# A modulation row written into the attention loop, and another way out of PSUM for the two halves of the attention output

## The chip, the cores and the metric

The kernel runs on one core of a Trainium2 chip. The metric is the device time of one execution in microseconds (us); the time of a kernel is the median of its runs. Five engines work side by side, each in the order of its own instruction queue: TensorE (PE in the profile; its weight loads are PEld), VectorE (DVE), ScalarE (ACT), GpSimd (POOL) and SyncE (SP), whose queue here issues most of the DMAs. Matmul results go to PSUM, everything else lies in SBUF.

## The reference

The reference is a two-layer encoder for one sequence of 1024 tokens and 1024 channels in fp32. Layer 0 has attention (16 query heads, 4 key and value heads of 64), layer 1 a Hyena convolution; both end in a feed-forward block with a depthwise convolution. What matters here is layer 0's modulation and its attention:

```python
mod = (c_act @ ada_w[i] + ada_b[i])[:, None, :]
sh1, sc1, g1, sh2, sc2, g2 = jnp.split(mod, 6, axis=-1)
h = rmsnorm(x, norm1_g[i]) * (1.0 + sc1) + sh1
...
s = jnp.einsum('bqkgd,bskd->bkgqs', q_blk, k, preferred_element_type=jnp.float32) * scale
p = jax.nn.softmax(s, axis=-1).astype(v.dtype)
return jnp.einsum('bkgqs,bskd->bqkgd', p, v)
...
x = x + g1 * y
h = rmsnorm(x, norm2_g[i]) * (1.0 + sc2) + sh2
x = x + g2 * conv_ffn(h, ...)
```

Of the six modulation rows of layer 0, `sh1` and `sc1` (rows 0 and 1) are needed before attention, `g1` (row 2) when attention's result is added to `x`, and rows 3 to 5 later still.

## The kernel before

**Number format.** An fp32 product is made of matmuls on fp32r parts: each operand is split into a high part (a cast on ScalarE) and a low part (the difference, a subtraction on VectorE, `sub_lo`, L162), and products of the parts are added up in PSUM.

**The projection (L757 to L792).** Queries, keys and values are computed in three chunks of 512 columns (`ch` 2, then 0, then 1), each for eight tiles of 128 tokens. TensorE fills a PSUM tile `qkv_mm`; VectorE and ScalarE normalise it and apply the rotary tables (`rope_norm`, L713 to L722, whose tiles are `qk_n`, `qk_a`, `qk_b`); TensorE transposes the result, and SP stores the queries to DRAM (`qd`). The weights come through two buffers called `w_raw`.

**Modulation rows on GpSimd.** `mod_step(i, acc, k)` (L185) loads 512 KB of `ada_w` into one of the same two `w_raw` buffers (SP, L187), multiplies it by a scalar per partition on GpSimd (L189 for k = 0, which writes `acc`; L191 otherwise) and adds it to `acc` (GpSimd, L192). `acc` is always the tile `ssq`. Eight steps make a row. `mod_fin` (L209) adds up `ssq` over the partitions with eight one-column matmuls (L212, 16 in the profile) and adds the bias on VectorE (`mod_bias`, L203); only then can the next row start to write `ssq`. Rows 0 and 1 and those of layer 1 are dot products on VectorE (`mod_dot`), the last of which read `ssq` as a row of activated conditions before row 2 begins. The eight steps of row 2 are written at the head of chunk `ch == 1` (L770).

**Attention (L811 to L938).** The work is cut into 32 units `u` (a key head g = u // 8 and a block of 128 queries, for the group's four query heads), each of eight key blocks `sb`. The loop counts `n` over all 256 pairs (u, sb), plus a lag of 2. Round n has, in written order:

- for sb = 0, `finish(u, 0)`: the reciprocal of the softmax sums (VectorE, L883), spread by GpSimd into `rbs` (L885);
- `transp` (TensorE transposes four tiles of probabilities into `pt_ps`, L854, three buffers), `pt_hi` (ScalarE, L859) and `pt_lo` (VectorE, L162, tile `pT_lo`);
- `attend` of the pair two rounds back: two matmuls into `o_ps` (L872, L873). `o_ps` has one buffer, a [128, 512] tile: the stationary operand `vst` holds high and low parts of the values side by side, so that partitions 0 to 63 get one half of the output and partitions 64 to 127 the other, and the output is their sum;
- when that pair was its unit's last, `finish(u, 2)` and `finish(u, 3)` (below);
- at set rounds a `mod_step` or a `mod_fin` for rows 3 to 5;
- for sb < 4, the scores of one head of the next unit: four matmuls into `s_ps` (L830, L831, two buffers), their row maximum `nmx` on VectorE (L838), the exponential `p_t` on ScalarE (L848).

`finish(u, 2)` moves both halves out of PSUM with four ScalarE copies of [64, 256] (L893): the even and the odd heads of the first half into the lower and the upper 64 partitions of `o_s`, the same of the second half into `o_l`. `finish(u, 3)` adds the two on VectorE (L895, [128, 256], both inputs in SBUF), transposes `rbs` into PSUM (L899, tile `rb_ps`), multiplies (VectorE, L900), and GpSimd writes high and low parts of the result (L902, L903).

**The order.** In the projection and in attention the queues are not ordered by hand. A scheduler builds the whole program at once: it takes written order as priority and lets every engine take the first instruction that can run by its own estimate of times. On each engine, on the chip, that order is then fixed.

**The rounds of the rows.** `LAG, MOD0, MODD = 2, 27, 9` (L905): with i, k = divmod((n - 27) // 9, 8), step k of row 3 + i is written at n = 27, 36, 45 and so on, one per nine key blocks, and `mod_fin` of a row six rounds after its last step: at n = 24 (row 2), 96, 168 and 240. At n = 246 the first weight tile of the output projection is loaded and split through `w_raw` (L927).

After attention, the output projection follows (`wo_y`), then the feed-forward block and layer 1.

Of the kernel before, what the change touches and what calls it, by code (L numbers as in the profile page):

```python
# [7 lines left out]
F32 = mybir.dt.float32  # L8
# [6 lines left out]
P = 128  # L15
D = 1024
L = 1024
KT = D // P
# [3 lines left out]
HD = 64  # L22
# [93 lines left out]
def tile_kernel(ctx: ExitStack, tc: tile.TileContext, t: dict):  # L116
    nc = tc.nc
    mm = nc.tensor.matmul
    V = nc.vector
    ADD, SUB, MUL = ALU.add, ALU.subtract, ALU.mult  # L120
# [64 lines left out]
    def mod_step(i, acc, k):  # L185
        raw = raw_tile()
        nc.sync.dma_start(raw, t["ada_w"][i - 2, k])  # L187
        if k == 0:
            nc.gpsimd.tensor_scalar(acc, raw, csil[:, 0:1], None, op0=MUL)  # L189
        else:  # L190
            nc.gpsimd.tensor_scalar(raw, raw, csil[:, k:k + 1], None, op0=MUL)  # L191
            nc.gpsimd.tensor_tensor(acc, acc, raw, op=ADD)  # L192
# [507 lines left out]
    with tc.tile_pool(name="qkv", bufs=1) as qp:  # L700
        def qtile(tag, bufs):
            return qp.tile([P, 8, HD], F32, name=tag, tag=tag, bufs=bufs)

        def stats(pv, nh):
            sq = qtile("qk_sq", 2)
            nc.scalar.activation(sq[:, 0:nh], pv, AF.Square)
            ss = qp.tile([P, 8], F32, name="qk_ss", tag="qk_ss", bufs=3)
            V.tensor_reduce(ss[:, 0:nh], sq[:, 0:nh], op=ADD, axis=AX.X)
            nc.scalar.activation(ss[:, 0:nh], ss[:, 0:nh], AF.Sqrt, bias=eps, scale=1.0 / HD)
            V.reciprocal(ss[:, 0:nh], ss[:, 0:nh])  # L710
            return ss

        def rope_norm(pv, nh, nm, j, ss):  # L713
            qn, A, B = qtile("qk_n", 2), qtile("qk_a", 2), qtile("qk_b", 2)
            V.tensor_tensor(qn[:, 0:nh], pv, ss[:, 0:nh].unsqueeze(2).to_broadcast([P, nh, HD]), op=MUL)
            V.tensor_tensor(A[:, 0:nh], qn[:, 0:nh], T[nm, 0][:, j:j + 1, :].to_broadcast([P, nh, HD]), op=MUL)
            for hf in range(2):
                a, b = slice(32 * hf, 32 * hf + 32), slice(32 - 32 * hf, 64 - 32 * hf)
                V.tensor_tensor(B[:, 0:nh, a], qn[:, 0:nh, b],
                                T[nm, 1][:, j:j + 1, a].to_broadcast([P, nh, 32]), op=MUL)  # L720
            V.tensor_tensor(A[:, 0:nh], A[:, 0:nh], B[:, 0:nh], op=ADD)
            return A  # L722

        def flat(ap):
            return ap.bitcast(F32).rearrange("p a d -> p (a d)")

        def k_tile(pv, ss, j):
            ts = slice(j * P, (j + 1) * P)
            nc.scalar.copy(vst[j][:, :, 0, :], pv[:, NKV:2 * NKV])
            sub_lo(vst[j][:, :, 1, :], pv[:, NKV:2 * NKV], vst[j][:, :, 0, :])  # L730
            kr = rope_norm(pv[:, 0:NKV], NKV, "k", j, ss)
            st = qp.tile([P, 2, NKV, 2, HD], F32R, name="k_st", tag="st", bufs=2)
            kin = kr[:, 0:NKV].unsqueeze(2)
            nc.scalar.copy(st[:, 0, :, 0:1, :], kin)
            sub_lo(st[:, 1, :, 0:1, :], kin, st[:, 0, :, 0:1, :])
            nc.scalar.copy(st[:, :, :, 1, :], st[:, :, :, 0, :].bitcast(F32))
            for i, dst in enumerate((kTh, kTl)):
                tp = mt("qkv_tr", "tr")
                for g in range(NKV):
                    nc.tensor.transpose(tp[:, g * P:(g + 1) * P], flat(st[:, i, g]), ident)  # L740
                for g in range(NKV):
                    nc.scalar.copy(dst[g][:, ts], tp[:, g * P:(g + 1) * P])

        def q_tile(pv, ss, j, ch):
            qr = rope_norm(pv, 8, "q", j, ss)
            st = qp.tile([P, 8, 2, HD], F32R, name="q_st", tag="st", bufs=2)
            nc.scalar.copy(st[:, :, 0, :], qr)
            sub_lo(st[:, :, 1, :], qr, st[:, :, 0, :])
            qs = qp.tile([P, 8, P], F32R, name="q_out", tag="q_out", bufs=1)
            for hf in range(2):  # L750
                tp = mt("qkv_tr", "tr")
                for i in range(4):
                    nc.tensor.transpose(tp[:, i * P:(i + 1) * P], flat(st[:, 4 * hf + i]), ident)
                nc.scalar.copy(qs[:, 4 * hf:4 * hf + 4, :], tp.rearrange("p (h q) -> p h q", q=P))
            nc.sync.dma_start(qd[ch][:, :, j * P:(j + 1) * P].rearrange("h p q -> p h q"), qs.bitcast(F32))

        todo = []  # L757
        silu_row(ssq)
        dots = mod_dots(0, L1_Q)

        def flush():
            if todo:
                todo.pop(0)()

        for ch in (2, 0, 1):
            w = qkv_w if ch == 2 else [load_split(t["w_qkv"][ch, k2], wq, 4) for k2 in range(4)]
            if ch == 1:
                for _ in dots:
                    pass
                for k in range(KT):  # L770
                    mod_step(2, ssq, k)
            pqs = dict(enumerate(pq0)) if ch == 2 else {}
            for j in range(NT):
                if j not in pqs:
                    pqs[j] = mt("qkv_mm", {2: "AAAABBAA", 0: "AABBAAAA", 1: "AAAABBBB"}[ch][j])
                    tj = slice(j * P, (j + 1) * P)
                    for k in range(KT):
                        wh, wl = w[k // 2]
                        cs = slice(512 * (k % 2), 512 * (k % 2) + 512)
                        mm3(pqs[j], hh[k][:, tj], hl[k][:, tj], wh[:, cs], wl[:, cs], k == 0, k == KT - 1)  # L780
                pv = pqs[j].rearrange("p (h d) -> p h d", d=HD)
                if ch == 0 or ch == 2 and j > 3:
                    next(dots, None)
                if ch == 2:
                    ss = stats(pv[:, 0:NKV], NKV)
                    flush()
                    todo.append(lambda pv=pv, ss=ss, j=j: k_tile(pv, ss, j))
                else:
                    ss = stats(pv, 8)
                    flush()  # L790
                    todo.append(lambda pv=pv, ss=ss, j=j, ch=ch: q_tile(pv, ss, j, ch))
        flush()  # L792
# [82 lines left out]
    fin = {}  # L875

    def finish(u, step):
        if u < 0:
            return
        g, qb = divmod(u, NT)  # L880
        if step == 0:
            rinv = at.tile([P, 4], F32, name="rinv", tag="rinv", bufs=2)
            V.reciprocal(rinv, sums[u])  # L883
            rbs = at.tile([P, 4, HD], F32, name="rbs", tag="rbs", bufs=3)
            nc.gpsimd.tensor_copy(rbs, rinv.unsqueeze(2).to_broadcast([P, 4, HD]))  # L885
            fin["rbs", u] = rbs.rearrange("p (a b) d -> p a (b d)", b=2)
        elif step == 2:
            fin["ol"] = at.tile([P, 2, P], F32, name="o_l", tag="o_l", bufs=2)
            fin["os"] = at.tile([P, 2, P], F32, name="o_s", tag="o_s", bufs=2)
            for lo, nm in ((0, "os"), (HD, "ol")):  # L890
                ov = o_t[u][lo:lo + HD, :].rearrange("p (a b q) -> p b a q", b=2, q=P)
                for par in range(2):
                    nc.scalar.copy(fin[nm][par * HD:(par + 1) * HD], ov[:, par])  # L893
        elif step == 3:
            V.tensor_tensor(fin["os"], fin["os"], fin["ol"], op=ADD)  # L895
            rb = ps.tile([P, 512], F32, name="rb_ps", tag="pt", bufs=3)
            fin["rb"] = rb[:, 0:256].rearrange("p (a q) -> p a q", q=P)
            for hp in range(2):
                nc.tensor.transpose(fin["rb"][:, hp], fin["rbs", u][:, hp], ident)  # L899
            V.tensor_tensor(fin["os"], fin["os"], fin["rb"], op=MUL)  # L900
            dst = [o_[:, 2 * g:2 * g + 2, qb * P:(qb + 1) * P] for o_ in (oht, olt)]
            nc.gpsimd.tensor_copy(dst[0], fin["os"])  # L902
            nc.gpsimd.tensor_tensor(dst[1], fin["os"], dst[0].bitcast(F32), op=SUB)  # L903

    LAG, MOD0, MODD = 2, 27, 9  # L905
    for u in range(3):
        load_q(u)
    for i in range(4):
# [4 lines left out]
    for n in range(len(steps) + LAG):  # L913
# [12 lines left out]
        if n == 246:  # L926
            w_o0 = load_split(t["w_o"][0], w0_pool, 1)  # L927
        i, k = divmod((n - MOD0) // MODD, KT)
        if (n - MOD0) % MODD == 0 and 0 <= i < 3:
            mod_step(3 + i, ssq, k)  # L930
        if (n - MOD0) % MODD == MODD - 3 and k == KT - 1 and -1 <= i < 3:
            mod_fin(0, 3 + i, ssq, lambda: ps.tile([P, 512], F32, name="pt_ps", tag="pt", bufs=3))
        if n < len(steps):
            u, sb = steps[n]
            if sb < 4 and u + 1 < NU:
# [1100 lines left out]
```

## Time and profile before

| | |
|---|---|
| median of 3 runs | 2940.22 us (2934.88 to 2940.23) |
| the profiled execution: time, span | 2945.4 us, 2943.4 us |
| its mean granted TensorE clock | 0.986 |
| busy: PE, DVE, ACT, POOL | 2819.3, 2330.6, 1232.5, 317.5 us |
| first and last attend matmul (L872, L873) | 234.4 and 628.6 us |
| first and last row step on GpSimd (L189, L192) | 155.4 and 546.7 us |

The profile is one execution, with times counted from the start of its span. A row of a timeline has the start and duration in us, engine, line, operation, output and inputs, and how many instructions were merged (x2); in brackets, how long the engine had been idle before and what ended that. A row of a group gives the count, total busy time in us and mean in ns, then the idle time ahead of the group's instructions with what ended it; a row of a tile gives minimum, median and maximum in ns, and the first and last start. A row of a stretch (two times with a colon) gives its length, each engine's busy time with the number of instructions, the granted clock, the DMA engines' busy share and GB/s.

### The profile page before, as it was taken

To read this page: it belongs to the slowest core of one execution; us is meant where nothing else is said; L and a number is where in the kernel's file an instruction comes from. 1 tells how busy PE (TensorE), PEld (TensorE's weight loads), DVE (VectorE), ACT (ScalarE), POOL (GpSimd) and SP (SyncE) were. 2 spreads that over 40 slices of the span, in tenths; PEclk is the share of its full clock that TensorE was granted. 3 is DMA by queue.
4 is the path that set the end of the run, shared out by engine and by line. 5 is a ranking of instruction groups with operands and counts; after the bars stand their busy time and mean duration, and the time that the engine had idled before them with its cause. 6 is when DMAs were issued, how large, how long until landed. Compare 5 with 4: busy or idle time off the path is not lost.

```text
span 2943.4 us, 36504 instructions
## 1 busy us (share of the span) xinstructions
PE 2819.3 (96%) x13152; PEld 2301.5 (78%) x13152; DVE 2330.6 (79%) x3225; ACT 1232.5 (42%) x1996; POOL 317.5 (11%) x344
## 2 busy tenths in 40 slices
PE   5989999999999999999999999999989999999998
PEld 4777877778888887888777887887868788887887
DVE  8797989869988887877777885888978887777544
ACT  3547888843444444343332332323334433333211
POOL 0063564400000000111000000000000000000000
PEclk9999999999999999999999999999999999999999
DMA  7262222146444444755456665556664332224321
GB/s 277 91 184 63 58 74 55 52 150 210 139 164 160 164 164 172 223 174 152 159 182 194 216 211 185 184 166 200 224 208 154 122 101 86 85 79 143 122 86 58
DMA packets 220823, 433.72 MB, mean 147 GB/s; under 512 B 22146, under 2 KB 117154, under 8 KB 216164
## 3 DMA queue, kind: packets, MB, share of 16 engines
q1 hardware_dynamic: 185444, 389.44, 39.5%
q0 software_dynamic: 35200, 41.95, 5.3%
q8 instruction: 104, 1.70, 0.2%
q14 instruction: 75, 0.61, 0.1%
HBM read 304.42 MB, written 126.89 MB: 147 GB/s over the span
## 4 chain that ended last, share of the span: by engine, by line
PE 64%; DVE 9%; DMA 4%; issue 1%; ACT 1%; SPq 0%; DVEq 0%; ACTq 0%; POOLq 0%
PE w_ps L1063 26%; PE d_ps L183 14%; PE u_ps L1437 4%; PE d_ps L1296 2%; PE wo_y L183 2%; PE ab_ps L1573 2%; PE f_ps L183 2%; PE g_ps L358 2%; PE v_ps L358 1%; DVE prod L1643 1%; PE f_ps L578 1%; PE wout_y L1859 1%; PE f_ps L579 1%; PE wo_y L1036 1%; DMA rd<-fw 1%
## 5 line engine op out<-in xcount | busy, mean ns | idle before, releaser
L1155 ACT CAST w_hi<-u 128x1024 fp32r<-128x1024 f32 x120 | 125.8, 1049 | 236.0 <-PE w_ps L1063 224.7
L162 DVE TENSOR_TENSOR pT_lo<-pt_ps,pT_hi 128x512 fp32r<-128x512 f32 x256 | 167.7, 681 | 46.9 <-ACT pT_hi L859 45.2
L1063 PE MATMUL w_ps<-t_h,w_hi 128*128 128x512 f32 x480 | 190.7, 397 | 1.9 <-ACT w_hi L1155 1.9
L1261 DVE SCALAR_TENSOR_TENSOR xd<-d_ps,mod,xd 128x1024 f32<-128x1024 f32 x104 | 132.7, 1280 | 75.4 <-PE d_ps L183 75.2
L1063 PE MATMUL w_ps<-t_h,w_lo 128*128 128x512 f32 x480 | 189.9, 397 | 0.7 <-DVE w_lo L162 0.7
L162 DVE TENSOR_TENSOR w_lo<-u,w_hi 128x1024 fp32r<-128x1024 f32 x120 | 146.6, 1222 | 55.6 <-ACT w_hi L1155 55.4
L1063 PE MATMUL w_ps<-t_l,w_hi 128*128 128x512 f32 x480 | 190.2, 396 | 0.0
L859 ACT CAST pT_hi<-pt_ps 128x512 fp32r<-128x512 f32 x256 | 145.0, 588 | 69.6 <-PE pt_ps L854 63.9
L183 PE MATMUL d_ps<-s_hi,wd_lo 128*128 128x512 f32 x544 | 170.0, 391 | 0.0
L183 PE MATMUL d_ps<-s_lo,wd_hi 128*128 128x512 f32 x544 | 169.9, 391 | 0.0
L183 PE MATMUL d_ps<-s_hi,wd_hi 128*128 128x512 f32 x544 | 168.9, 390 | 0.0
L838 DVE TENSOR_REDUCE nmx<-s_ps 128x1 f32<-128x1024 f32 x128 | 155.5, 1217 | 10.8 <-PE s_ps L831 9.0
L854 PE MATMUL pt_ps<-ident,p_t 128*128 128x128 f32 x1024 | 154.4, 274 | 10.0 <-DVE pT_lo L162 9.0
L854 PEld LDWEIGHTS pt_ps<-ident,p_t 128*128 128x128 f32 x1024 | 126.6, 141 | 44.8 <-DVE pT_lo L162 7.8
L848 ACT ACTIVATE p_t<-s_ps,nmx 128x1024 f32<-128x1024 f32 x128 | 143.7, 1124 | 3.9 <-DVE nmx L838 2.7
L1437 PE MATMUL u_ps<-fh_h,w_lo 128*128 128x512 f32 x368 | 132.5, 419 | 2.4 <-DMA w_lo<-wld 2.4
L1573 PE MATMUL ab_ps<-prod,dfti 128*128 128x256 f32 x512 | 124.7, 387 | 6.8 <-DVE prod L1643 3.4
L1437 PE MATMUL u_ps<-fh_l,w_hi 128*128 128x512 f32 x368 | 127.8, 414 | 0.0
L1063 PE MATMUL w_ps<-fh_h,w_hi 128*128 128x512 f32 x320 | 124.9, 390 | 0.7 <-ACT w_hi L1155 0.7
L1063 PE MATMUL w_ps<-fh_l,w_hi 128*128 128x512 f32 x320 | 124.8, 390 | 0.0
L1063 PE MATMUL w_ps<-gh_h,w_hi 128*128 128x512 f32 x320 | 124.7, 390 | 0.0
L1063 PE MATMUL w_ps<-gh_l,w_hi 128*128 128x512 f32 x320 | 124.7, 390 | 0.0
(424 smaller groups left out, 7556.3 us busy)
## 6 DMA issues: line engine op xcount, KB each, us to landing
u<-in_w_up_dram SPq DMA_DIRECT2D x80, 512.0 KB
w_raw<-in_w_down_dram SPq DMA_DIRECT2D x44, 512.0 KB
sg<-gate SPq DMA_DIRECT2D x40, 512.0 KB
w_raw<-sg SPq DMA_DIRECT2D x40, 512.0 KB
w_raw<-in_ada_w_dram SPq DMA_DIRECT2D x32, 512.0 KB
ed<-eo SPq DMA_DIRECT2D x64, 256.0 KB
eo<-ed SPq DMA_DIRECT2D x16, 1024.0 KB
kd<-k_sb SPq DMA_DIRECT2D x64, 256.0 KB
```

What stands on the lines that cost most here:

```text
L162: V.tensor_tensor(lo, src, hi.bitcast(F32), op=SUB)
L183: mm(out[:, cs], lhsT=a, rhs=b[:, cs], start=start and i == 0, stop=stop and i == 2)
L358: mm(pp[:, HS[hf]], lhsT=(wh, wh, wl)[i][:, ks], rhs=hd[hf][i % 2][k], start=k == 0 and i == 0, stop=k == n - 1 and i == 2)
L838: V.tensor_reduce(nmx, s_t[u, i], op=ALU.max, axis=AX.X, negate=True)
L848: nc.scalar.activation(p_t, s_ps, AF.Exp, bias=nmx, accum_out=sums[u][:, i:i + 1])
L854: nc.tensor.transpose(tp[:, i * P:(i + 1) * P], pts[u, i][:, sb * P:(sb + 1) * P], ident)
L859: nc.scalar.copy(ph, pt_t[u, sb][0])
L1063: mm(out, lhsT=(w[0], w[0], w[1])[i][:, k * P:(k + 1) * P], rhs=b[i % 2][k], start=k == 0 and i == 0, stop=k == 3 and i == 2)
L1155: nc.scalar.copy(w[0], src)
L1261: ins = V.scalar_tensor_tensor(x[dt_], yp, gate[dt_], x[dt_], op0=MUL, op1=ADD)
L1437: mm(yp[:, HS[hf]], lhsT=(wh, wh, wl)[i][:, k * P:(k + 1) * P], rhs=hd[hf][i % 2][k], start=k == 0 and i == 0, stop=k == KT - 1 and i == 2)
L1573: mm(ap[:, i], lhsT=dfti[:, m, :], rhs=v, start=n == 0, stop=n == len(ops) - 1)
```

## The change

Row 2 goes into the attention loop: the eight steps at L770 are deleted, and the loop now serves four rows, 2 to 5, from n = 21 on with one step per seven rounds, k-th step of row 2 + i at n = 21 + 56 i + 7 k. `mod_fin` is written four rounds after a row's last step: at n = 74, 130, 186 and 242.

`finish(u, 2)` now copies only the second half, partitions 64 to 127, with one ScalarE copy of [64, 512] into the lower 64 partitions of `o_l` (one buffer in place of two). Two VectorE additions of [64, 256] then read the first half from PSUM and `o_l` from SBUF, one for the even heads (into the lower 64 partitions of `o_s`) and one for the odd (into the upper). The addition in `finish(u, 3)` is gone.

```diff
             if ch == 1:
                 for _ in dots:
                     pass
-                for k in range(KT):
-                    mod_step(2, ssq, k)
...
         elif step == 2:
-            fin["ol"] = at.tile([P, 2, P], F32, name="o_l", tag="o_l", bufs=2)
+            ol = at.tile([HD, 512], F32, name="o_l", tag="o_l", bufs=1)
             fin["os"] = at.tile([P, 2, P], F32, name="o_s", tag="o_s", bufs=2)
-            for lo, nm in ((0, "os"), (HD, "ol")):
-                ov = o_t[u][lo:lo + HD, :].rearrange("p (a b q) -> p b a q", b=2, q=P)
-                for par in range(2):
-                    nc.scalar.copy(fin[nm][par * HD:(par + 1) * HD], ov[:, par])
+            nc.scalar.copy(ol, o_t[u][HD:P, :])
+            oa, ob = [o_.rearrange("p (a b q) -> p b a q", b=2, q=P) for o_ in (o_t[u][0:HD, :], ol)]
+            for par in range(2):
+                V.tensor_tensor(fin["os"][par * HD:(par + 1) * HD], oa[:, par], ob[:, par], op=ADD)
         elif step == 3:
-            V.tensor_tensor(fin["os"], fin["os"], fin["ol"], op=ADD)
             rb = ps.tile([P, 512], F32, name="rb_ps", tag="pt", bufs=3)
...
-    LAG, MOD0, MODD = 2, 27, 9
+    LAG, MOD0, MODD = 2, 21, 7
...
         i, k = divmod((n - MOD0) // MODD, KT)
-        if (n - MOD0) % MODD == 0 and 0 <= i < 3:
-            mod_step(3 + i, ssq, k)
-        if (n - MOD0) % MODD == MODD - 3 and k == KT - 1 and -1 <= i < 3:
-            mod_fin(0, 3 + i, ssq, lambda: ps.tile([P, 512], F32, name="pt_ps", tag="pt", bufs=3))
+        if (n - MOD0) % MODD == 0 and 0 <= i < 4:
+            mod_step(2 + i, ssq, k)
+        if (n - MOD0) % MODD == MODD - 3 and k == KT - 1 and 0 <= i < 4:
+            mod_fin(0, 2 + i, ssq, lambda: ps.tile([P, 512], F32, name="pt_ps", tag="pt", bufs=3))
```

## The prediction

> **What bounds the kernel now.** I read the page first, then busy time by stretch (windows) over the two stages that the change touches, then the timelines of those stages and the groups by tile. In attention:
>
> ```profile
> core 0: us, PE busy (x) PEld busy (x) DVE busy (x) ACT busy (x) POOL busy (x), PEclk, DMA share, GB/s
> 354.18:365.67 11.49, 11.49 (x68) 9.28 (x66) 10.41 (x16) 10.11 (x21) 2.33 (x4) 1.00 0.12 24
> 270.85:284.61 13.76, 11.64 (x68) 9.32 (x66) 12.16 (x15) 8.69 (x17) 11.25 (x8) 1.00 0.35 97
> 379.83:394.75 14.92, 12.94 (x68) 10.54 (x67) 12.01 (x14) 8.68 (x17) 11.48 (x9) 0.89 0.32 89
> 489.73:503.52 13.79, 11.67 (x67) 9.32 (x66) 12.20 (x15) 8.70 (x17) 11.27 (x8) 1.00 0.33 95
> ```
>
> These four stretches run from one unit's `rb_ps` transposes (L899) to the next unit's, so each is one unit of 8 key blocks. The first is the ordinary unit: 11.49 us, TensorE busy all of it. The other three follow a `mod_fin`; TensorE has the same work (68 matmuls) and about 2 us without any, while GpSimd (POOL) is busy. One of them in detail:
>
> ```profile
> 267.24 1.84 PE L212 MATMUL pt_ps<-ones,ssq 128*128 128x1 f32 x16
> 269.19 2.85 POOL L189 TENSOR_SCALAR ssq<-w_raw,csil 128x1024 f32<-128x1024 f32 x1 [6.02 <-PE pt_ps L212]
> 271.18 1.21 DVE L838 TENSOR_REDUCE nmx<-s_ps 128x1 f32<-128x1024 f32 x1
> 272.31 3.21 DVE L895 TENSOR_TENSOR o_s<-o_s,o_l 128x256 f32<-128x256 f32 x1
> 272.84 2.39 POOL L192 TENSOR_TENSOR ssq<-ssq,w_raw 128x1024 f32<-128x1024 f32 x1
> 276.18 0.66 PE L854 MATMUL pt_ps<-ident,p_t 128*128 128x128 f32 x4 [1.97 <-DVE pT_lo L162]
> ```
>
> When `mod_fin` has read `ssq`, GpSimd starts the next row. The addition of the value halves (L895) meets GpSimd's work and takes 3.21 us, ending when GpSimd's L192 does; VectorE (DVE) is in order, the `pT_lo` behind it is late, and TensorE waits 1.97 us. Over the stage:
>
> ```profile
> L895 DVE TENSOR_TENSOR o_s<-o_s,o_l 128x256 f32<-128x256 f32 x32 | 28.7, 896 | 3.1 <-ACT o_l L893 3.1
> L895 DVE TENSOR_TENSOR o_s<-o_s,o_l x32: 415/417/3220, 247.8 to 630.9; 128x256 f32<-128x256 f32 x32
> L900 DVE TENSOR_TENSOR o_s<-o_s,rb_ps x32: 391/420/423, 249.2 to 631.4; 128x256 f32<-128x256 f32 x32
> L162 DVE TENSOR_TENSOR pT_lo<-pt_ps,pT_hi x256: 652/681/693, 234.4 to 627.9; 128x512 fp32r<-128x512 f32 x128
> ```
>
> L895 has both inputs in SBUF: median 417 ns, worst 3220. L900 and `pT_lo` have one input in PSUM: in 288 runs beside the same GpSimd work their worst is 423 and 693. Only the first kind is stalled.
>
> **The change, part by part.** *The stall goes.* The new additions have one input in PSUM, like L900, so GpSimd shouldn't stall them. The three units above exceed 11.49 by 2.27 + 3.43 + 2.30 = 8.0 us, all behind this stall: **-8.0 us**. L895's whole excess is 28.7 - 32 x 0.417 = 15.4 us; the three long ones take 3 x 2.8 = 8.4 of it, 7.0 is left in shorter ones. One of these, with its unit:
>
> ```profile
> 429.30 0.38 PE L899 MATMUL rb_ps<-ident,rbs 128*128 128x128 f32 x2
> 431.82 1.37 DVE L895 TENSOR_TENSOR o_s<-o_s,o_l 128x256 f32<-128x256 f32 x1
> 441.12 0.38 PE L899 MATMUL rb_ps<-ident,rbs 128*128 128x128 f32 x2
> ```
>
> Its 0.95 us of stall made the unit 11.82, 0.33 over; the rest was covered by matmuls already fed. At a third, 7.0 us gives **-2.0** (bounds 0 and -7.0).
>
> *The handover of `o_ps`.* There is one `o_ps` buffer, and it is now free after one copy on ScalarE (ACT) and two additions, instead of four copies. An ordinary unit's boundary:
>
> ```profile
> 365.43 0.40 PE L873 MATMUL o_ps<-pT_lo,vst 128*128 128x512 f32 x1
> 365.86 1.28 DVE L162 TENSOR_TENSOR pT_lo<-pt_ps,pT_hi 128x512 fp32r<-128x512 f32 x2
> 365.93 0.74 ACT L893 COPY o_s<-o_ps 64x256 f32<-64x256 f32 x2
> 366.70 0.75 ACT L893 COPY o_l<-o_ps 64x256 f32<-64x256 f32 x2
> 366.82 0.82 PE L854 MATMUL pt_ps<-ident,p_t 128*128 128x128 f32 x6
> 367.06 1.22 DVE L838 TENSOR_REDUCE nmx<-s_ps 128x1 f32<-128x1024 f32 x1
> 367.50 0.50 PE L872 MATMUL o_ps<-pT_hi,vst 128*128 128x512 f32 x1
> 368.07 0.38 PE L854 MATMUL pt_ps<-ident,p_t 128*128 128x128 f32 x2
> 368.19 0.41 DVE L895 TENSOR_TENSOR o_s<-o_s,o_l 128x256 f32<-128x256 f32 x1
> L859 ACT CAST pT_hi<-pt_ps 128x512 fp32r<-128x512 f32 x256 | 145.0, 588 | 69.6 <-PE pt_ps L854 63.9 <-DMA qd<-q_out 2.3 <-PE o_ps L872 0.4
> ```
>
> Today the copies last from 365.93 to 367.45 and the next unit's first attend starts at 367.50: the handover is on TensorE's path. The new copy moves 512 columns out of PSUM, as L859 does: 0.59 us. The additions are priced at L900's 0.42, and an op can start 0.08 before the one ahead ends (L895 at 272.31 under `nmx`, which ends at 272.39), so 0.33 after one of that size. If VectorE takes them at once, `o_ps` is free 0.59 + 0.05 + 0.33 + 0.42 = 1.39 us after the copy's start, 0.13 sooner than now. But these additions queue on VectorE, and TensorE waits behind them: after the second `pT_lo` of 365.86, which occupies it until 367.06, they end at 367.81, 0.36 later than now; behind `nmx`, 1.1 us from start to the next op, up to 1.0 later. Two transposes that now follow (L854 x2, 0.14 us) can fill the gap. Per unit that is -0.13 to +0.86; I take +0.11, the mean of the first case at nothing and the second at 0.36 - 0.14, in 30 units: **+3.3 us** (bounds -4 and +26). On the engines themselves ScalarE loses 1.49 - 0.59 = 0.9 us a unit and VectorE gains 0.33, with 10.1 and 10.4 of 11.49 busy: free as long as TensorE's 11.49 is longer, and each unit stays below it. `o_l` with one buffer waits for additions of a unit earlier: nothing.
>
> [...]
>
> *The tail.* Behind attention's last matmul nothing covers the chain:
>
> ```profile
> 629.24 0.74 ACT L893 COPY o_s<-o_ps 64x256 f32<-64x256 f32 x2 [1.38 <-PE o_ps L873]
> 630.85 0.43 DVE L895 TENSOR_TENSOR o_s<-o_s,o_l 128x256 f32<-128x256 f32 x1 [2.27 <-ACT o_l L893]
> 631.95 0.76 PE L183 MATMUL wo_y<-oh,w_hi 128*128 128x512 f32 x1 [2.81 <-DVE o_s L900]
> ```
>
> Copies to first addition take 1.61 us, which becomes 0.59 + 0.1, plus 0.33 for the second addition: **-0.6**.
>
> *The moved row.* Row 2's eight steps (a 512 KB load on SP and two GpSimd ops each) are written later, after the projection. Does GpSimd run them later?
>
> ```profile
> 145.00:212.00 67.00, 20.79 (x7) 0.97 0.67 189
> 212.00:234.37 22.37, 2.84 (x1) 0.79 0.52 141
> 216.91 0.53 SPq L187 DMA_DIRECT2D w_raw<-in_ada_w_dram  x1
> 234.37 0.50 PE L872 MATMUL o_ps<-pT_hi,vst 128*128 128x512 f32 x1 [1.55 <-ACT pT_hi L859]
> 284.61 0.38 PE L899 MATMUL rb_ps<-ident,rbs 128*128 128x128 f32 x2
> 296.20 0.38 PE L899 MATMUL rb_ps<-ident,rbs 128*128 128x128 f32 x2
> ```
>
> The first two rows give GpSimd's busy time in L191 and, in brackets, how many ran: seven are row 2's, all in the projection. The eighth, before attention's first attend at 234.37, is row 3's second step. It is written at n = 36, which lies between the L899 of u = 3 (n = 33, 284.61) and u = 4 (n = 41, 296.20), near 289, and its load went out at 216.91, when a `w_raw` buffer came free. So SP and GpSimd get a step as soon as its buffer and data allow, some 70 us before its written place. Row 2's first step will find the buffers free at the same moment as now, behind the same `w_qkv` loads, and `ssq` has long been read by the dots. It stays, I expect, in the projection, with its stalls: **0**. What really moves is `mod_fin`, which TensorE keeps in written order: row 2's from n = 24 to 74, the others from 96, 168 and 240 to 130, 186 and 242. Four are in attention before and after: 0 (to 2 us either way by what they fall beside). Eight steps are 8 x (2.85 + 2.39) = 42 us of GpSimd in the 56 x 1.44 = 80 us between fins (1.44 is 11.49 / 8), so no `mod_fin` should wait for its row, and the SP loads have no other load to pass there.
>
> Sum: -8.0 - 2.0 + 3.3 - 0.6 = -7.3 us. The profiled execution took 2945.4 us (span 2943.4), 5.2 above the runs' median of 2940.22; -7.3 gives 2938.1 on its scale and **2932.9 us** on the median's.
>
> **Rivals.** *The row does leave the projection.* For: counted from n = 33 at 284.61, n = 21 falls near 267 and n = 70 near 338; to run between 145 and 212 as now it must be some 120 us ahead, farther than the 70 seen. Against: nothing in the trace limits the lead but buffers and data. Its price:
>
> ```profile
> 190.00:226.00 36.00, 27.64 (x121) 21.74 (x120) 33.55 (x38) 20.71 (x36) 21.16 (x9) 0.81 0.56 166
> 226.00:240.00 14.00, 10.80 (x53) 8.03 (x52) 7.87 (x11) 7.61 (x14) 1.53 (x3) 0.88 0.37 95
> L719 DVE TENSOR_TENSOR qk_b<-qk_n,Tq x32: 411/418/3105, 116.7 to 218.8; 128x256 f32<-128x256 f32 x32
> ```
>
> The rope products (L719) show the same stall, 418 to 3105 ns, and TensorE is idle for 8.4 + 3.2 = 11.6 us at a clock of 0.81 to 0.88. Most of it, 10 us, would go: 2923.
>
> *The handover eats the gain.* At +0.3 us a unit, the `pT_lo` case throughout: 9 instead of 3.3, net -1.6, 2939: no change.
>
> *Slower.* The additions land behind `nmx` in every unit, as L895 does now at 368.19, harmlessly because `o_ps` is already free. Then 0.86 us x 30 = 26 against 10.6 gained: +15, 2955. It decides from 0.55 us a unit. Against it: the copy ends 0.9 us sooner than `o_l` does, before `nmx` starts, and the additions are written ahead of it.
>
> **How the numbers follow.** Forecast (2930 to 2937) 45%; row leaves the projection (2919 to 2927) 20%; gain eaten (2935 to 2942) 16%; slower 19%. A measurement tells 0.2% from no change here, 5.9 us: 2934.3 and below is faster. Two thirds of the forecast's 45 lie there, with the 20: 51% faster; 14 + 16 = 30% the same; 19% slower. The range of 2920 to 2945 leaves out most of the slower case and the edge of the first rival; the forecast's own is 2930 to 2937.
>
> **What would show it.** Right: no VectorE addition of `o_s` over 0.5 us; units after a `mod_fin` back at 11.5 to 11.7; seven L191 still before 212 us; ordinary units at 11.5 to 11.7. Wrong: GpSimd idle of L191 before 234 us with TensorE's idle time there gone (first rival), or ordinary units above 12 us with `o_ps` matmuls waiting for VectorE's additions (the slower one).

## The result, and the profile after

The changed kernel takes 2970.45 us (median; 2970.07 to 2970.78) against 2940.22 for the kernel before on the same chip: a ratio of 1.0098, with a 95% interval of 1.0085 to 1.0111, so some 30 us slower. The forecast was 2932.9 us, in a range of 2920 to 2945. The profiled execution took 2970.07 us, with a span of 2968.3 (before: 2945.4 and 2943.4), at a granted clock of 0.988 (before 0.986).

Two steps of the prediction can be checked at once. GpSimd's busy time in the multiplications of the rows (L191) over the two stretches shown for before, now in the kernel after:

```profile
145.00:212.00 67.00, 21.15 (x7) 0.97 0.65 189
212.00:234.37 22.37, 2.95 (x1) 0.85 0.52 141
```

Seven again before 212 us and one behind: row 2 has stayed in the projection. Then the new additions (L891), by tile, and the groups of the evacuation between 230 and 660 us:

```profile
L891 DVE TENSOR_TENSOR o_s<-o_ps,o_l x64: 402/417/419, 248.4 to 661.9; 64x256 f32<-64x256 f32 x64
L888 ACT COPY o_l<-o_ps 64x512 f32<-64x512 f32 x31 | 18.0, 582 | 19.2 <-PE o_ps L871 19.1
L852 PE MATMUL pt_ps<-ident,p_t 128*128 128x128 f32 x1024 | 154.3, 274 | 23.2 <-DVE pT_lo L162 22.2 <-ACT q_out L754 1.0
```

The longest of 64 additions takes 419 ns, where the old one took up to 3220: the stalls under GpSimd are gone. The copy takes 0.58 us. But TensorE's transposes now wait 22.2 us for VectorE's `pT_lo` (9.0 before), and every ordinary unit is longer. One of them as a stretch, from `rb_ps` to `rb_ps` as before:

```profile
297.75:310.75 13.00, 11.94 (x68) 9.44 (x67) 10.76 (x17) 9.46 (x17) 2.23 (x5) 1.00 0.11 21
```

It lasts 13.00 us instead of 11.49. TensorE is idle for about 1.05 of it; the other 0.45 lies in what the profile counts as busy, 11.94 us for 68 matmuls that took 11.49 before (the ends of matmuls are modelled, so the first part of a wait can count as busy). Its timeline, with the rows that answer to the boundary shown for before:

```profile
297.52 0.39 PE L871 MATMUL o_ps<-pT_lo,vst 128*128 128x512 f32 x1
297.75 0.38 PE L896 MATMUL rb_ps<-ident,rbs 128*128 128x128 f32 x2
297.95 0.58 ACT L888 COPY o_l<-o_ps 64x512 f32<-64x512 f32 x1 [0.68 <-PE o_ps L871]
298.07 1.28 DVE L162 TENSOR_TENSOR pT_lo<-pt_ps,pT_hi 128x512 fp32r<-128x512 f32 x2
298.89 0.63 PE L852 MATMUL pt_ps<-ident,p_t 128*128 128x128 f32 x4 [0.76 <-DVE pT_lo L162]
299.27 1.21 DVE L836 TENSOR_REDUCE nmx<-s_ps 128x1 f32<-128x1024 f32 x1
299.82 0.50 PE L828 MATMUL s_ps<-kTh,q_t 128*128 128x512 f32 x1 [0.29 <-ACT p_t L846]
300.40 0.83 DVE L891 TENSOR_TENSOR o_s<-o_ps,o_l 64x256 f32<-64x256 f32 x2
300.86 0.60 PE L852 MATMUL pt_ps<-ident,p_t 128*128 128x128 f32 x4
301.26 0.69 DVE L162 TENSOR_TENSOR pT_lo<-pt_ps,pT_hi 128x512 fp32r<-128x512 f32 x1
301.38 0.47 PE L870 MATMUL o_ps<-pT_hi,vst 128*128 128x512 f32 x1
```

Two things have changed. First, the additions start at 300.40, 1.87 us after the copy's end at 298.53: in VectorE's queue they stand behind two `pT_lo` and the row maximum `nmx`. `o_ps` is free at 301.23, 3.28 us after the copy began; before, the copies took 1.52. Second, TensorE does its work in another order. Between the last attend of a unit (297.52) and the first of the next (301.38) it now has a score product and eight transposes, where it had a score product and six. Five attend matmuls follow in a row, and late in the unit two score products stand one behind the other. Written as letters (t a transpose, s a score matmul, o an attend matmul, R an `rb` transpose), the ordinary unit's queue on TensorE was, and is:

```
before  ssss tttttt oo tt oo ssss o tttt o tttt o ssss o tttt oo tttt oo tttt o ssss o tttt oo RR
after   tttt ssss tttt ooooo ssss tttt oo tttt o tttt oo tttt oo tttt oo tttt ssss ssss oo RR
```

*Where the time went.* From the first `rb` transposes to the last, attention takes 659.28 - 245.79 = 413.5 us, before 627.77 - 245.16 = 382.6. The 24 ordinary units have 12.99 us each where 11.48 was usual, 24 x 1.51 = 36.2 us more. Attention less 24 ordinary units is 101.7 us, before 107.1: 5.4 less, a remainder that holds the stalls and also the other layout of the units with a `mod_fin` and of the last ones. The rest of the span behind the last `rb` is 2309.0 us, before 2315.6. In the kernels below, whose code there is the same, it lies between 2311.6 and 2323.2, so this term is taken as scatter and was not followed up.

### The profile page after: what moved, and what is told of

Same layout as the page of the kernel before. It is cut to its first block, busy times and chain, and to the rows that moved or that the text cites. A ratio compares the mean times of both kernels' runs of the same rounds, so it can differ in the third digit from the quotient of the medians.

```text
span 2968.3 us, 36401 instructions
## 1 busy us (share of the span) xinstructions
PE 2825.3 (95%) x13152; PEld 2302.9 (78%) x13152; DVE 2325.4 (78%) x3257; ACT 1209.7 (41%) x1900; POOL 313.5 (11%) x344
## 4 chain that ended last, share of the span: by engine, by line
PE 77%; DVE 12%; DMA 6%; ACT 3%; issue 2%; SPq 0%; DVEq 0%; ACTq 0%; POOLq 0%
PE w_ps L1060 26%; PE d_ps L183 14%; PE u_ps L1434 5%; PE pt_ps L852 3%; PE o_ps L871 2%; PE qkv_mm L183 2%; PE o_ps L870 2%; PE s_ps L828 2%; PE d_ps L1293 2%; PE s_ps L829 2%; PE wo_y L183 2%; PE ab_ps L1570 2%; PE f_ps L183 2%; PE g_ps L358 1%; PE f_ps L578 1%
## 5 line engine op out<-in xcount | busy, mean ns | idle before, releaser
L852 PE MATMUL pt_ps<-ident,p_t 128*128 128x128 f32 x1024 | 154.3, 274 | 23.2 <-DVE pT_lo L162 22.2
L846 ACT ACTIVATE p_t<-s_ps,nmx 128x1024 f32<-128x1024 f32 x128 | 142.2, 1114 | 11.3 <-DVE nmx L836 7.7
```

The costliest lines, as they stand in the source:

```text
L846: nc.scalar.activation(p_t, s_ps, AF.Exp, bias=nmx, accum_out=sums[u][:, i:i + 1])
L852: nc.tensor.transpose(tp[:, i * P:(i + 1) * P], pts[u, i][:, sb * P:(sb + 1) * P], ident)
```

## The experiments

Two theories at first. *Handover*: the late release of `o_ps` costs the 1.5 us a unit. *Order*: the other queue order does, whoever frees `o_ps`. A third, *rows*, lays it on the moved row and the new spacing. In some kernels the queues of TensorE, VectorE and ScalarE in attention are held to a given order, by ordering edges between neighbours that bring no wait with them:

```diff
+    for e, order in ORDER.items():
+        row = [kinds[e, c].pop(0) for c in order]
+        for i, j in zip(row, row[1:]):
+            tc.add_manual_dep(j, i.name, mybir.DependencyInfo(mybir.DependencyClass.NoSync, mybir.DependencyReason.DATA),
+                              reason="order")
```

`ORDER` has one letter for each instruction; on VectorE l is `pT_lo`, n the row maximum, a an addition, m the multiplication and r the reciprocal, on ScalarE c is a copy, e an exponential and h `pT_hi`. In the old order an ordinary unit of VectorE is `m ll n r ll n ll n ll n a`, in the new one `m r l n llll n ll n aa l n`.

### Each half of the change alone

`e1_rows_only` has the new rows with the old evacuation, `e2_copies_only` the new evacuation with the old rows:

```diff
             if ch == 1:
                 for _ in dots:
                     pass
-                for k in range(KT):
-                    mod_step(2, ssq, k)
...
-    LAG, MOD0, MODD = 2, 27, 9
+    LAG, MOD0, MODD = 2, 21, 7
```

is e1 against the kernel before (with the loop's four rows), and e2 against it is

```diff
-            for lo, nm in ((0, "os"), (HD, "ol")):
...
+            nc.scalar.copy(ol, o_t[u][HD:P, :])
...
+            for par in range(2):
+                V.tensor_tensor(fin["os"][par * HD:(par + 1) * HD], oa[:, par], ob[:, par], op=ADD)
...
-            V.tensor_tensor(fin["os"], fin["os"], fin["ol"], op=ADD)
```

> The new rows of the modulation (row 2 in the loop, one step per seven key blocks), with the evacuation of before (four ScalarE copies, one addition from SBUF). Theory 1, handover: the two additions that free o_ps come late on VectorE and that alone costs 1.5 us a unit; then ordinary units are back at 11.5 us here and the time is 2930 to 2944. Theory 2, order: the scheduler laid TensorE, VectorE and ScalarE out in another order around the new evacuation, with two score products back to back at the end of each unit, and that order costs the 1.5 us whoever frees o_ps; this kernel's order is mostly that of before, so again 11.5 us a unit and 2930 to 2944. Theory 3, rows: the moved row and the new spacing cost it; then 13.0 us a unit or a long wait elsewhere, 2970.

> The new evacuation (one copy, two additions from PSUM) with the rows of before (three rows in the loop, every nine blocks). Handover and order: units of 13.0 us as in the changed kernel, since both the late release and the paired score products are there; 2965 to 2975. Rows: 11.5 us a unit and 2930 to 2938.

Measured: e1 2937.53 us, ratio 0.9982 (0.9973 to 0.9991), ordinary units 11.47. e2 2966.78 us, ratio 1.0081 (1.0066 to 1.0096), ordinary units 12.99. The rows alone make the kernel slightly faster; the theory of the rows falls, and the evacuation has the whole loss. The scheduler gave e1 the old order in its ordinary units and e2 the new one, so these two can't part the other theories.

### Old and new order, exchanged

`e5_new_evac_old_order` holds the changed kernel to e1's order, `e6_old_evac_new_order` holds e1 to the changed kernel's. Of `ORDER`, the ordinary unit on the three engines; first e5, which has `c` and `aa` where e1 has `cccc` and `a`:

```diff
+        + "ssssttttttoottoossssottttottttossssottttoottttoottttossssottttooRR" * 5
...
+        + "llnrllnllnllnaam" * 5
...
+        + "ehhehhhehehhc" * 6
```

then e6, which has `cccc` and `a` where the changed kernel has `c` and `aa`:

```diff
+        + "ttttssssttttooooossssttttoottttottttoottttoottttoottttssssssssooRR" * 6
...
+        + "rlnllllnllnalnm" * 6
...
+        + "ehehhhheehhhcccc" * 26
```

> The changed kernel, with TensorE, VectorE and ScalarE held to the order in which the kernel with the old evacuation (e1_rows_only) issues attention: the one copy stands where the four stood, the two additions where the one stood, behind the row maximum. Order: units of 11.5 to 11.7 us, 2925 to 2938. Handover by the time that the release takes: the additions end 0.86 us later than the fourth copy did, 12.3 us a unit, 2950 to 2958. Handover as it was measured in the changed kernel: 13.0, 2970.

> The kernel of e1_rows_only (old evacuation, new rows) held to the order of the changed kernel on the three engines; ScalarE alone frees o_ps here. Order: 13.0 us a unit, 2965 to 2980. Handover: no unit waits for VectorE's addition, 11.5 us a unit, 2930 to 2944.

Measured: e5 2984.31 us, 1.0138 (1.0122 to 1.0154); e6 2993.68 us, 1.0169 (1.0152 to 1.0186). Both are slower than the changed kernel and than every expected range. An ordinary unit of e1, e5 and e6, in this order:

```profile
301.09:312.56 11.47, 11.47 (x68) 9.28 (x67) 10.40 (x16) 10.06 (x21) 2.31 (x4) 1.00 0.12 24
```
```profile
311.34:324.40 13.06, 11.53 (x68) 9.35 (x67) 11.20 (x17) 9.46 (x18) 2.31 (x4) 1.00 0.11 21
```
```profile
326.86:340.49 13.63, 11.59 (x68) 9.47 (x66) 10.57 (x16) 10.29 (x20) 2.21 (x5) 1.00 0.11 20
```

In the old order the new evacuation costs 1.56 us a unit; in the new order the unit is long even with the old evacuation, and longer than in the changed kernel. At the boundary of e5's unit:

```profile
324.59 1.28 DVE L212 TENSOR_TENSOR pT_lo<-pt_ps,pT_hi 128x512 fp32r<-128x512 f32 x2
324.78 0.58 ACT L938 COPY o_l<-o_ps 64x512 f32<-64x512 f32 x1
325.79 1.22 DVE L886 TENSOR_REDUCE nmx<-s_ps 128x1 f32<-128x1024 f32 x1
326.92 0.84 DVE L941 TENSOR_TENSOR o_s<-o_ps,o_l 64x256 f32<-64x256 f32 x2
327.90 0.47 PE L920 MATMUL o_ps<-pT_hi,vst 128*128 128x512 f32 x1 [1.54 <-DVE o_s L941]
```

The first attend comes 3.12 us after the copy's start; in e1 it comes 1.56 after the start of the first of four copies. The difference is the 1.56 that the unit is longer by: TensorE's 1.54 of idle time, put down to the addition.

### The release of `o_ps`, moved

Three kernels in the old order. In `e7_add_before_nmx` the additions stand ahead of the row maximum, in `e8_add_between_lows` one place further ahead; in `e9_two_copies_old_order` they stand as in e5, but ScalarE alone frees `o_ps`:

```diff
-        + "llnrllnllnllnaam" * 5
+        + "llnrllnllnllaanm" * 5
```

for e7,

```diff
-        + "llnrllnllnllnaam" * 5
+        + "llnrllnllnlaalnm" * 5
```

for e8, and for e9

```diff
-            fin["os"] = at.tile([P, 2, P], F32, name="o_s", tag="o_s", bufs=2)
+            fin["os"] = at.tile([P, 2, P], F32, name="o_s", tag="o_s", bufs=1)
             nc.scalar.copy(ol, o_t[u][HD:P, :])
+            oh_ = at.tile([HD, 512], F32, name="o_h", tag="o_h", bufs=1)
+            nc.scalar.copy(oh_, o_t[u][0:HD, :])
-            oa, ob = [... for o_ in (o_t[u][0:HD, :], ol)]
+            oa, ob = [... for o_ in (oh_, ol)]
```

(`...` stands for the same `rearrange` as before; `o_s` has one buffer here in place of two, in e4 and e11 too.)

> As e5_new_evac_old_order, but the two additions stand ahead of the row maximum on VectorE, right behind the two pT_lo. Handover: in e5 o_ps is freed 1.7 us later than in e1_rows_only, of which the row maximum is 1.13; without it the additions end about 0.5 us later than the fourth copy did, so 11.9 to 12.0 us a unit, 2944 to 2954. Rival, VectorE's added work (0.42 us a unit) and not the time of release: no change to e5, 13.0 us a unit, 2980. Rival, the order of the row maximum: it comes 0.84 us later, and if that is what score products wait for, 12.4 us or more a unit, 2958 or more.

> As e7, with the two additions one place further ahead, between the two pT_lo. Handover: the copy ends 0.59 us after its start and the additions 0.86 us later, the same moment at which the fourth copy ended: 11.5 to 11.7 us a unit, 2930 to 2942. Rival, VectorE's added work: 13.0 us a unit, 2980. Rival, the later pT_lo and row maximum: 12.0 to 12.4, 2950 to 2960.

> Two ScalarE copies of 64x512 take both halves out of o_ps, and the two additions read SBUF alone; the order is that of e1_rows_only, additions behind the row maximum as in e5. VectorE has the same work as in e5. Handover: ScalarE frees o_ps after 1.17 us instead of 1.49, 11.2 to 11.5 us a unit, 2928 to 2938, with a few additions stalled by GpSimd (0.9 to 3.2 us). Rival, VectorE's added work: 13.0 us a unit, 2980.

Measured: e7 2946.89 us, 1.0012 (1.0000 to 1.0024), units of 11.90. e8 2962.46, 1.0065 (1.0050 to 1.0081), units of 12.50. e9 2956.74, 1.0042 (1.0026 to 1.0058), units of 11.27. The boundary in e7:

```profile
304.20 0.58 ACT L938 COPY o_l<-o_ps 64x512 f32<-64x512 f32 x1
305.20 0.84 DVE L941 TENSOR_TENSOR o_s<-o_ps,o_l 64x256 f32<-64x256 f32 x2
306.19 0.47 PE L920 MATMUL o_ps<-pT_hi,vst 128*128 128x512 f32 x1 [0.41 <-DVE o_s L941]
```

and in e9, where the additions come after the attend that would have waited for them:

```profile
307.76 0.59 ACT L938 COPY o_l<-o_ps 64x512 f32<-64x512 f32 x1
308.36 0.58 ACT L940 COPY o_h<-o_ps 64x512 f32<-64x512 f32 x1
309.10 0.48 PE L920 MATMUL o_ps<-pT_hi,vst 128*128 128x512 f32 x1
309.89 0.84 DVE L943 TENSOR_TENSOR o_s<-o_h,o_l 64x256 f32<-64x256 f32 x2
```

From the start of the first copy to the next attend it is 1.34 us in e9, 1.56 in e1, 1.99 in e7 and 3.12 in e5; the ordinary units are 11.27, 11.47, 11.90 and 13.03. Each step of the unit is the step of the release, within 0.02. e5 and e9 have the same instructions on VectorE in the same order, so its added work is not the cause: in the old order the handover theory holds, to the size. e8 is a miss for it: its additions end at 309.74, 1.53 us after the copy's start, yet its unit is 1.03 longer than e1's. There the second `pT_lo` and the row maximum come 1.0 us later after the copy's start than in e1, and TensorE waits for that `pT_lo` in the middle of the six transposes:

```profile
310.61 0.41 PE L902 MATMUL pt_ps<-ident,p_t 128*128 128x128 f32 x2 [1.05 <-DVE pT_lo L212]
```

This is the rival that named the later `pT_lo`. It had the place right and was nearest, though 12.50 us is just outside its range. None of the three places tried on VectorE is free for additions that hold `o_ps`.

e9's total is some 20 us above what its ordinary units promised. Its additions read SBUF alone again:

```profile
L943 DVE TENSOR_TENSOR o_s<-o_h,o_l 64x256 f32<-64x256 f32 x64 | 47.2, 738 | 3.0 <-ACT o_h L940 2.6
386.15:399.65 13.50, 11.60 (x68) 9.26 (x66) 12.94 (x17) 9.83 (x19) 7.56 (x6) 1.00 0.36 98
```

47.2 - 64 x 0.418 = 20.4 us of stalls, in units such as the second row's, where GpSimd is busy for 7.56 us.

### The order by itself

`e4_two_copies` has e9's two copies, with the order left to the scheduler. `e10_after_order_add_first` is the changed kernel held to its own order, but with the additions ahead of the row maximum:

```diff
-        + "rlnllllnllnaalnm" * 6
+        + "rlnllllnllaanlnm" * 6
```

(e10 against the changed kernel's own order; e4 has e9's diff without an `ORDER`.)

> The same two ScalarE copies, with the order left to the scheduler, which here alternates: every second unit has the order of the changed kernel (two score products back to back at its end), the others one like that of before. Handover alone: all units 11.2 to 11.6 us, 2930 to 2940. Order as a cost of its own, as e6 says: every second unit 12.9 to 13.3 us, 2950 to 2962.

> The changed kernel held to its own order on the three engines, with one thing moved: the two additions stand ahead of the row maximum instead of behind it, as e7 did in the old order. If the late release of o_ps is what makes a unit 13.0 us in the changed kernel's own order too, it falls to 12.0 us or less, 2940 to 2950. If the order that the scheduler laid around the late release is bound elsewhere (two transposes and a score product stand ahead of the first attend there, and TensorE waits 1.0 us for VectorE's pT_lo and ScalarE's exponential in it), it stays at 12.9 to 13.2 us, 2965 to 2980.

Measured: e4 2982.71 us, 1.0134 (1.0117 to 1.0152), its first units 12.69 and 12.89 in turn. On TensorE the units of 12.89 have the new order and those of 12.69 a third one, not that of before as was expected; both are long. e10 2974.9 us, 1.0097 (1.0074 to 1.0119), units of 12.99. At e10's boundary:

```profile
297.52 0.58 ACT L929 COPY o_l<-o_ps 64x512 f32<-64x512 f32 x1 [0.69 <-PE o_ps L912]
298.46 0.63 PE L893 MATMUL pt_ps<-ident,p_t 128*128 128x128 f32 x4 [0.76 <-DVE pT_lo L203]
298.83 0.84 DVE L932 TENSOR_TENSOR o_s<-o_ps,o_l 64x256 f32<-64x256 f32 x2
299.38 0.50 PE L869 MATMUL s_ps<-kTh,q_t 128*128 128x512 f32 x1 [0.30 <-ACT p_t L887]
300.78 0.48 PE L911 MATMUL o_ps<-pT_hi,vst 128*128 128x512 f32 x1
```

`o_ps` is free at 299.67, 1.57 us after the copy's end where the changed kernel needs 2.70, and the attend still comes at 300.78, behind the same transposes and the same score product. In the new order an earlier release alone wins nothing. The ordinary units side by side, in us:

| evacuation | old order | new order |
|---|---|---|
| four copies | 11.47 (e1) | 13.63 (e6) |
| two copies | 11.27 (e9) | 12.89 (e4, every second one of its first units; the others, 12.69, have the third order) |
| copy, additions ahead of `nmx` | 11.90 (e7) | 12.99 (e10) |
| copy, additions behind `nmx` | 13.03 (e5) | 12.99 (the changed kernel) |

The late release costs 1.56 us with the old order; the new order costs 1.1 to 2.2 with an evacuation that is quick in the old one; together they cost no more than one of them.

### What closes the loop in the new order

Three kernels in the changed kernel's own order, with one swap each: `e13_after_order_low_first` moves a `pT_lo` ahead of the row maximum that holds it back, `e14_after_order_exp_first` an exponential ahead of the copy of `o_l` on ScalarE, `e15_after_order_exp_apart` sets two exponentials apart as well:

```diff
-        + "rlnllllnllnaalnm" * 6
+        + "rlnlllllnlnaalnm" * 6
```

is e13. On ScalarE, e14 and e15 in turn:

```diff
-        + "ehehhhheehhhc" * 26
+        + "hehhhheehhhec" * 29
```
```diff
-        + "hehhhheehhhec" * 29
+        + "hehhhhehehhec" * 29
```

> The changed kernel held to its own order on the three engines, with one thing moved: of the two pT_lo that stand behind the third row maximum of a unit, one goes ahead of it. In the changed kernel TensorE waits 0.76 us in each unit, right behind the rb transposes, for a pt_ps buffer that the pT_lo behind that row maximum frees, and 0.29 us for an exponential. If the order costs its 1.5 us through the buffer of pt_ps, the unit falls to 12.2 to 12.6 us, 2946 to 2960. If the loop closes through the row maximum, the exponential and the score products, which come 0.65 us later here, it stays at 13.0 us or rises to 13.6, 2970 to 2988.

> The changed kernel held to its own order, with one swap on ScalarE: the exponential that stands behind the copy of o_l goes ahead of it. The row maximum ends 0.4 us before the copy does, so the exponential can start 0.4 us sooner. If the chain from the unit's last attend over the copy to the exponential and the next score product closes the loop, TensorE's wait of 0.29 us for that exponential goes: 12.6 to 12.75 us a unit, 2958 to 2966; the copy and the additions end no later, as the additions wait for the row maximum anyway. If not, 12.9 to 13.1.

> As e14, and one pT_hi goes between the two exponentials that follow one another late in the unit. VectorE sits idle for 2.2 us before the pT_lo that waits for it, and the row maximum and the two pT_lo behind that pT_lo hold up TensorE's transposes for 0.76 us. If that closes the loop, 12.2 to 12.5 us a unit, 2944 to 2958. If the row maximum there waits for its score product instead, which waits for the second exponential, now 0.58 us later, 12.7 to 13.2.

Measured: e13 2980.32 us, 1.0131 (1.0106 to 1.0156), units of 12.99; e14 2969.42 us, 1.0088 (1.0070 to 1.0106), 12.98; e15 2964.19 us, 1.0070 (1.0054 to 1.0087), 12.64. In e13 the wait for `pT_lo` is gone and the wait for the exponential has grown:

```profile
299.90 0.60 PE L893 MATMUL pt_ps<-ident,p_t 128*128 128x128 f32 x4
301.93 0.50 PE L869 MATMUL s_ps<-kTh,q_t 128*128 128x512 f32 x1 [1.43 <-ACT p_t L887]
```

In e14 the wait for the exponential is gone, and `o_ps` makes TensorE wait instead:

```profile
295.95 0.63 PE L890 MATMUL pt_ps<-ident,p_t 128*128 128x128 f32 x4 [0.76 <-DVE pT_lo L200]
298.43 0.47 PE L908 MATMUL o_ps<-pT_hi,vst 128*128 128x512 f32 x1 [0.30 <-DVE o_s L929]
```

In e6, where four copies stand ahead of that exponential on ScalarE, TensorE waits longer for it:

```profile
329.90 0.50 PE L869 MATMUL s_ps<-kTh,q_t 128*128 128x512 f32 x1 [1.28 <-ACT p_t L887]
```

So no single wait sets the 13 us: TensorE's idle time moves between `pT_lo`, the exponential and `o_ps` (1.05 us in the changed kernel, 1.06 in e14, 1.43 in e13), and these units stay at 12.98 to 12.99. Only e15, which also cuts the first wait to 0.31 us (0.30 are left for `o_ps`), gains, 0.34 us; that lies between the two cases expected of it.

The profile's critical view shows why. It follows the work back through what released each step; its rows have start, duration, engine, tile and line. Through an ordinary unit of the changed kernel it leaves TensorE only here:

```profile
297.68 0.25 PE o_ps L871
297.95 0.58 ACT o_l L888
298.56 1.21 ACT p_t L846 x2
299.82 0.50 PE s_ps L828
```

The unit's last attend releases the copy, the exponential stands behind the copy in ScalarE's queue, and the next score product waits for the exponential. In e10 the chain is the same; in e6 four copies stand ahead of that exponential; in e13 the row maximum, later there, holds it back in the copy's place. In e14, with the exponential ahead of the copy, the chain goes over VectorE instead (rows selected):

```profile
305.75 0.59 ACT pT_hi L895
306.36 0.29 DVE pT_lo L200
306.97 1.21 DVE nmx L874
308.18 1.20 DVE pT_lo L200 x2
309.38 0.71 DVE nmx L874
310.43 0.40 DVE o_s L929
310.85 0.43 DVE o_s L929
311.41 0.47 PE o_ps L908
```

This second chain ends in the additions and the release of `o_ps`, and the changed kernel is at its limit too: its first attend starts 0.15 us after the additions end, as in e14, and 0.19 after the start of the transpose ahead of it, where that step is 0.03 in e10. So two chains of about the same length hold the unit at 12.99. e10 relieves only the second and e14 only the first, and neither gains; e15 relieves the first, shortens the second, and gains. Why the two are equally long, which order would win all of the 1.5 us, and why the scheduler's estimate takes the one order for four copies and the other for one were not tried.

### A kernel that keeps the gain and not the loss

`e11_best` joins e9's copies and the old order with the old rows, and spaces the steps so that GpSimd's work doesn't meet the additions. `e12_old_copies_spaced` does the same with the old evacuation:

```diff
-    LAG, MOD0, MODD = 2, 27, 9
+    LAG, MOD0, MODD = 2, 26, 8
...
-            nc.gpsimd.tensor_copy(rbs, rinv.unsqueeze(2).to_broadcast([P, 4, HD]))
+            fin["b"] = nc.gpsimd.tensor_copy(rbs, rinv.unsqueeze(2).to_broadcast([P, 4, HD]))
...
-            mod_step(3 + i, ssq, k)
+            with tc.issue_after(fin["b"].ins):
+                mod_step(3 + i, ssq, k)
```

> Two ScalarE copies of 64x512 as in e9, the ordinary unit's order of e1_rows_only in units 2 to 27, and the rows of before (three in the loop) at one step per eight blocks, which is one per unit, each step's GpSimd operations held behind that unit's copy to rbs, so that they end before the next unit's additions. Handover: ordinary units of 11.3 us, no addition over 0.5 us, three units with a mod_fin of about 14.5; e9's attention of 394 us less the 27 that its stalled units take gives 367 against 383 before: 2922 to 2932. If e9's long units are not stalls by GpSimd, they stay: 2940 to 2957.

> As e11, but with the evacuation of before (four copies, one addition from SBUF). Handover: ScalarE frees o_ps 0.33 us later than in e11, ordinary units of 11.5 us, 0.2 more than in e11, 6 us in all: 2928 to 2938. If only the stalls matter, no difference to e11.

Measured: e11 2924.52 us, 0.9931 (0.9916 to 0.9946); e12 2934.21 us, 0.9971 (0.9959 to 0.9984). e11's additions, and one of its units with a row step in it:

```profile
L921 DVE TENSOR_TENSOR o_s<-o_h,o_l x64: 406/418/421, 247.7 to 611.1; 64x256 f32<-64x256 f32 x64
302.00:313.30 11.30, 11.30 (x68) 9.36 (x67) 10.74 (x17) 9.82 (x19) 7.63 (x7) 1.00 0.26 70
```

GpSimd is busy for 7.63 us of this unit, no addition is over 421 ns, TensorE never stops. From the first `rb` to the last it is 362.8 us in e11, 369.9 in e12 and 382.6 before: 12.7 us for the spacing and the fixed order together, 7.1 for the earlier release, where 6 was expected. The units with a `mod_fin` were expected at 14.5 us and take 12.9; here no stall follows it (the next units take 11.3). e11 is faster than both kernels.

## Why the prediction was wrong, step by step

- *The stall goes, -8.0 and -2.0.* Right as a mechanism: no addition over 0.42 us, and the units that follow a `mod_fin` are as long as any other (12.99 us at 364.53, 458.84 and 551.59). As a sum it is somewhat off. In the second of the three units (379.83) TensorE itself is busy for 12.94 us, where it is 11.64 and 11.67 in the others, at a granted clock of 0.89: 1.3 of the 8.0 us are the slower clock and no stall. The changed kernel has such a unit too (442.45 to 458.84, clock 0.90). And a third of 7.0 is 2.3, not 2.0. What the stalls were worth in all can't be read off, as the remainder of 5.4 us above holds other things as well. Part of it was to be had without the new evacuation: e1 has 6.4 us of stalls instead of 15.4, and is 4.5 us faster than before.
- *The tail, -0.6.* Right: from the last attend matmul to the first `wo_y` behind it 660.14 to 662.87, 2.73 us, where it was 628.64 to 631.95, 3.31.
- *The moved row, 0.* Right in place: it stayed in the projection. The rival in which it leaves fell with that.
- *The handover, +3.3.* **This is the step that failed**, with three errors. The first is the value taken, +0.11 a unit: a mean of "at once" and "behind one `pT_lo`", though the row in which the old addition stands behind `nmx` (368.19) was in the prediction itself. "Written ahead of it" was no protection: the scheduler put the additions behind `nmx`, probably because they depend on the copy and `nmx` is ready sooner by its estimate (argued, not tried). e7 shows the `pT_lo` case at 0.43 (0.22 in the sum, 0.3 in the rival that eats the gain), 0.41 of it idle time on TensorE; the transposes that were to fill 0.14 of it filled nothing.
- *The upper bound, +0.86.* The second error is in the sum itself: `nmx`'s 1.13 us were added to the case "at once" (-0.13) and not to the `pT_lo` case, behind which `nmx` starts (+0.36). 0.36 + 1.13 = 1.49; less the 0.14 for the filled gap it is 1.35, and 30 units less 10.6 gained give +30, not +15. e5 measures 1.56. So the slower rival had the right mechanism for the old order and about half its price. That +30 is what the changed kernel loses proves nothing, since it loses it in another order.
- *What was not in the prediction at all* is the third: that the scheduler lays out TensorE's, VectorE's and ScalarE's queues anew around another evacuation. Each price was read at the boundary of an ordinary unit on the assumption that the rest of the unit stays in place. It didn't, and the new order costs as much as the late release: e4 and e9 have the same instructions, and their units differ by 1.4 to 1.6 us. ScalarE's copy was priced by busy time ("free as long as TensorE's 11.49 is longer"), but in the new order it lies on the chain from the last attend to the next score product. Of the two signs that the prediction names for the slower case, the units above 12 us are in the profile. The `o_ps` matmuls that wait for additions hardly are: 301.38 has no idle time ahead of it, and comes some 0.16 us later than its transposes alone would let it.

The handover also counted 0.33 + 0.42 us for the two additions, the second starting 0.08 us before the first ends. In the changed kernel the first starts 0.08 before the end of `nmx` (300.40 against 300.48), but the second starts at 300.81, 0.01 after the first's end; the two together take 0.83 us, twice 0.417, and the next `pT_lo` starts at 301.26, 0.03 after their end. At about 0.2 us a unit it is a small part of 1.5. The trace of before has one more such row, outside attention: a memset that writes partitions 64 to 127 (L131, at 1.04 us), as the second addition does, starts some 0.045 us after the end of the op ahead of it, and the next op as long after its own end. No run shows what sets this.

## What to carry to other kernels

When an operation that frees a buffer moves to another engine, price it from its place in that engine's queue, summing all that stands ahead of it; where its input comes late, price the case behind the longest op as well, which is the one that came true here. Look at what it holds up on its own engine too (e8), and at what stands behind the op that stays (the exponential behind the copy). Where a scheduler lays out the queues, compare the two queue orders of the steady loop before believing any price read at one place: with the order free, two copies in place of four made the ordinary unit 1.2 to 1.4 us longer (e4 against e1), and with the order held the same edit won 0.2 us a unit (e9). When relieving one wait only moves it to another, look for a second chain of the same length. A loop that fills TensorE completely is worth holding in place first.

## What the runs showed of the hardware that was not expected

Two additions in the place of one met GpSimd's work more often where both operands lie in SBUF: with the same rows and spacing, e9 has 20.4 us of stalls over 64 additions (seven take over 2.6 us, the longest 4.4), and e1 some 6.4 over 32 (four long ones: two of 1.37 and two of 2.64 us). With one operand in PSUM, 64 additions beside the same rows stayed at 402 to 419 ns. e11 fits this: with GpSimd's steps in another part of the unit, 64 additions from SBUF took 406 to 421 ns.
